# A hybrid decoder block on one core: the attention's second score product over 128 rows instead of 64

## The chip, the cores and the metric

The kernel runs on one core of a Trainium2 chip. The metric is the device time of one execution in microseconds (us); the median of three runs before the change is 2642.2 us (2641.92 to 2643.72). Lower is better. The core's engines are TensorE (PE in the profile, its weight loads PEld), VectorE (DVE), ScalarE (ACT), GpSimd (POOL) and SyncE (SP), which here only issues DMAs.

## The reference

One layer over 1024 tokens of width 1024, in float32. A mixer with two branches (stick-breaking attention and a gated linear recurrence, HGRN2), merged by gates, projected and normalized; then a mixture of experts (32 experts, 4 a token) and a second norm. The change concerns the attention's scores alone:

```python
for blk in range(T // SB_BLOCK):                 # 8 blocks of 128 queries, 8 heads of 64 channels
    t0, t1 = blk * SB_BLOCK, (blk + 1) * SB_BLOCK
    z = einsum('bhtd,bhsd->bhts', qf[:, :, t0:t1], kf[:, :, :t1]) * scale
    mask = arange(t1)[None, :] < (t0 + arange(SB_BLOCK))[:, None]
    log_keep = where(mask, log_sigmoid(-z), 0.0)
    log_after = cumsum(log_keep, axis=3, reverse=True) - log_keep
    weights = where(mask, exp(log_sigmoid(z) + log_after), 0.0)
    outs.append(einsum('bhts,bhsd->bhtd', weights, vf[:, :, :t1]))
```

## The kernel before

The program runs in stages, one after another: input projections, the recurrence beside some projections, the projections for the attention, the attention, the merge of the branches, the output projection with the router, the experts, the last norm. TensorE's float32 products are made from parts: each operand is split into a high and a low part of 12 bits (`split`, L124 to L126), and three products (high by high, high by low, low by high) are summed in one bank.

The attention is `sb_attention` (L557). A unit of work is one block of 128 queries for some heads: all 8 heads in block 0, 4 in block 1, 2 in blocks 2 and 3, and one head in blocks 4 to 7. There are 43 units, and block i has 128 * (i + 1) keys. A unit passes through four steps, one unit further behind in each: `scores` (matmuls L611 and L612, then on ScalarE a sigmoid of both signs, L615 and L616, then on GpSimd the mask, L620), `stick` (on VectorE a running product L629 and a product L631), `turn` (transposes on TensorE L642, copies L645 or L647) and `average` (matmuls L664 against the values).

The scores of a head take three part products, made in two matmuls for each stretch of up to 512 keys. A head has 64 channels, half of the 128 partitions. The tile `q` (`split_q`, L572) has the high part of a head's queries on the head's own half of the partitions and the low part on the other half; `kh` has the high part of its keys on both halves. So L611, over all 128 rows, makes high by high and low by high at once. What is left, queries high by keys low, is L612: it takes only the head's own 64 rows of `q` and of `kl`, in which two heads lie one below the other:

```python
r = slice(64 * (h % 2), 64 * (h % 2) + 64)
nc.tensor.matmul(o, q[:, h], self.kh[:, h, s], start=True, stop=False)
nc.tensor.matmul(o, q[r, h], self.kl[r, h // 2, s], start=False, stop=True)
```

So in a unit of one head with more than 512 keys four score matmuls follow one another, of 128, 64, 128 and 64 rows; with 8 heads in block 0 there are 16.

The queries come from DRAM. `load_q(i)` (L566) issues two DMAs on the SP queue into a tile `qraw`, of which there are two buffers. The first unit loads block 0 and block 1; every later block's first unit loads the next block. `split_q` (ScalarE copy L576, two VectorE subtractions L579) of the next block comes late in a block (in block 0 in its only unit, ahead of that unit's matmuls). The order in which instructions are written is the order on each engine.

Beside the attention runs a second stream of work, `beside` in `block_kernel` (L1643): first six pieces of the gates' projection (matmuls L130 to L132, 512 columns each; copies L548; weight loads on the SP queue L225, split by L125 and L126), then `turn_branches` (L696), which turns the branches' outputs (transposes L730, splits L125 and L126) once the memory of the projection has been given up. `lockstep` (L70) puts the two streams into one order by the estimated TensorE time that each piece yields. This order is fixed when the program is written, and does not hang on what the chip does.

Of the kernel before, what the change touches and what calls it, by code (L numbers as in the profile page):

```python
# [69 lines left out]
def lockstep(*streams):  # L70
    """Emits generators side by side; each yields the tensor-engine time of the piece it emitted."""
    total = [0.0] * len(streams)
    live = set(range(len(streams)))
    weight = [w for _, w in streams]
    gens = [g for g, _ in streams]
    while live:
        i = min(live, key=lambda j: total[j] / weight[j])
        try:
            total[i] += next(gens[i])
        except StopIteration:  # L80
            live.discard(i)


def shape_constants():
    """Arrays of zeros and ones that hang on the shapes alone."""
# [29 lines left out]
class Block:  # L115
# [56 lines left out]
    def scratch(self):  # L172
        """Expert lists in DRAM: (token, gate) by expert and place; at first every place names a zero row."""
        nc = self.nc
        self.tab_d = self.dram("tab_scratch", (NE * ROWS, 2), I32)
        self.h_d = self.dram("h_scratch", (ROWS, D))
        self.acc_d = self.dram("acc_scratch", (ROWS, D))
        n = NE * ROWS // 128
        for i in range(2):
            t = self.work.tile([128, n], I32, name="E0", bufs=EBUFS[0])  # L180
            nc.sync.dma_start(t, self.a["c_tab"][:, n * i:n * i + n])
            nc.gpsimd.dma_start(self.tab_d.rearrange("(p r) c -> p (r c)", p=128)[:, n * i:n * i + n], t)
        z = self.work.tile([128, 512], F32, name="E0", bufs=EBUFS[0])
        nc.gpsimd.memset(z, 0.0)
        for d in (self.h_d, self.acc_d):
            for half in range(2):
                nc.gpsimd.dma_start(d[T:T + 128, 512 * half:512 * half + 512], z)

# [1 line left out]
    def load_x(self):  # L190
        nc, a = self.nc, self.a
        # by half of the tokens
        self.xh = [p.tile([128, KT, 512], F32R, name=f"xh{i}") for i, p in enumerate(self.xpool)]
        self.xl = [p.tile([128, KT, 512], F32R, name=f"xl{i}") for i, p in enumerate(self.xpool)]
        # the place of q and f, which come later, takes the rows
# [21 lines left out]
    def fetch(self, col):  # L217
        """Loads columns col..col+256 of w_in and splits them."""
# [10 lines left out]
    def project(self, jobs, ahead=None):  # L229
        """jobs: (column, halves, evacuate): 256 columns by channel for these halves of the tokens, or by token for  # L230
        all of them where halves is None. A generator over pieces of tensor-engine work.

        ahead: a generator whose steps come before those of the first job.
        """
# [62 lines left out]
    def hgrn_jobs(self):  # L297
        """Projections of the HGRN branch: q^T and f^T by channel, v and the output gate by token."""
# [43 lines left out]
    def hgrn_chunks(self):  # L342
        """Chunks of 128 tokens: one chunk's decays beside the scores of the one before."""
# [17 lines left out]
    def hgrn_front(self, c, state):  # L361
        """Log gates of a chunk, their sums over ranges of tokens, and what these scale."""
# [15 lines left out]
        # q beside what the odd tokens' q keeps of the token before  # L378
# [10 lines left out]
        # decays from each token to the chunk's end  # L389
# [7 lines left out]
        for g, n in enumerate((4, 3)):  # L397
            for h in range(NH):
# [6 lines left out]
                for i in range(n):  # L405
# [5 lines left out]
                    # the first half of each block takes k, the second q  # L411
# [7 lines left out]
    def hgrn_back(self, c, state):  # L419
        """Scores within a chunk, its output, and the state it leaves."""  # L420
# [8 lines left out]
        # a token with itself and with the one before  # L429
# [52 lines left out]
    def rsqrt(self, pool, v, scale, eps, n):  # L482
        """1 / sqrt(v * scale + eps), with a Newton step on the table's value."""
# [14 lines left out]
    def sb_tiles(self):  # L498
        sp = self.spool
        # the first part of a head's keys lies on both halves of the partitions  # L500
        self.kh = sp.tile([128, SBH, T], F32R, name="kh")
        self.kl = sp.tile([128, 4, T], F32R, name="kl")
        self.sv = sp.tile([128, NB, 512], F32, name="sv")

    def sb_jobs(self):
        """q^T, kept in DRAM, k^T in two parts, v by token."""
# [33 lines left out]
    def gates_jobs(self):  # L540
        """The merge gates' arguments, by channel, kept in DRAM until the merge; a part of them early, a part late."""
# [15 lines left out]
    def sb_attention(self):  # L557
        """Weights sigmoid(z_s) * prod over s < s' < t of sigmoid(-z_s'), s < t."""
        nc, wk = self.nc, self.work
        self.os_d = self.dram("osb_scratch", (T, 512))  # L560
        # a unit is a head's block of queries, or several heads' where the keys are few
# [4 lines left out]
        def load_q(i):  # L566
            raw = wk.tile([128, SBH, 128], F32, name="qraw", bufs=2)
# [4 lines left out]
        def split_q(i):  # L572
            # the first part on the head's own partitions, the second on the others
# [7 lines left out]

        def heads(u):
            # those on the same half of the partitions follow one another: their products share a bank
# [4 lines left out]
        def scores(u):  # L588
            i, h0 = units[u]
            m, S = HEADS[i], 128 * (i + 1)  # L590
            if u == 0:
                load_q(i)
                split_q(i)
            if i in after and h0 == 0:
# [8 lines left out]
            for g in range(0, m, per):  # L603
                for s0 in range(0, S, 512):
                    n = min(512, S - s0)
                    ps = self.sps.tile([128, 512], F32, name="z", bufs=2)
                    for k in range(per):
                        h = hs[g + k]
                        r = slice(64 * (h % 2), 64 * (h % 2) + 64)
                        o, s = ps[:, S * k:S * k + n], slice(s0, s0 + n)  # L610
                        nc.tensor.matmul(o, q[:, h], self.kh[:, h, s], start=True, stop=False)  # L611
                        nc.tensor.matmul(o, q[r, h], self.kl[r, h // 2, s], start=False, stop=True)  # L612
# [4 lines left out]
            # a token keeps all of what itself and later ones would take  # L617
# [35 lines left out]
        def average(u):  # L653
            # two heads side by side, by channel
# [41 lines left out]
    def turn_branches(self):  # L696
        """The branches' outputs by channel, in two parts."""
# [4 lines left out]
        # the stick-breaking branch is there by channel: its own place in memory takes it  # L702
# [107 lines left out]
    def layer_norm(self, pool, r, st, g, b, out):  # L810
        """From the statistics of both halves of the rows."""
# [9 lines left out]
    def outproj(self):  # L821
# [6 lines left out]
        # the first part of the biases twice and the second, one below the other  # L828
# [33 lines left out]
        def add(tb, half):  # L862
            """The residual, and the statistics of what results."""
# [5 lines left out]
        def project(tbs):  # L869
            """Blocks of tokens; two at a time follow the loading of the weights row block by row block."""  # L870
# [26 lines left out]
        def route(tb):  # L897
# [10 lines left out]
            # four sums side by side, by expert, then their sum by token  # L908
# [17 lines left out]
            # which experts each token takes, and with what weight  # L926
# [31 lines left out]
            # places within the experts' lists  # L958
# [26 lines left out]
            # what the experts' outputs are added to: the residual and the weighted biases  # L985
# [36 lines left out]
        # then the last block first: the order of the experts waits for it  # L1022
# [11 lines left out]
    def expert_constants(self):  # L1034
        """What the sorting needs, and the biases in two parts, the second below the first."""
# [15 lines left out]
    def sort_experts(self):  # L1051
        """Each expert's place in the order of the counts."""
# [4 lines left out]
        # distinct keys: the count, then the lower expert first  # L1057
# [23 lines left out]
    def sort_biases(self):  # L1081
        nc, cp = self.nc, self.epool
        # biases of the first product, by channel and place in the order
# [11 lines left out]
    def list_beyond(self):  # L1095
        """What lies beyond the static sizes: blocks of 128 places, listed."""
# [15 lines left out]
        # row of an expert's first block beyond, less 128 for each block listed before  # L1112
# [4 lines left out]
        # one block a partition: its expert and its first row  # L1117
# [15 lines left out]
        # the same along a row  # L1133
# [14 lines left out]
    # Two forms of an expert's product. Up to 128 places: the tokens are the stationary operand and the  # L1148
    # weights stream past. More: the weights are stationary and both parts of the tokens stream past them.

    def expert(self, n, e, rows, bias, choice):
# [38 lines left out]
        def fetch(kind, c, q, width, queue=nc.sync, e=e):  # L1190
            """2048 weights a partition: a chunk of columns, blocks of rows from q * kr on."""
# [5 lines left out]
        def part(kind, c, q, width, kn):  # L1197
            """Piece q of a chunk of columns, kn blocks of rows, in two parts."""
# [156 lines left out]
        # pieces of work: the load of weights that starts with it, their split, the product, what follows a little later  # L1355
# [21 lines left out]
    def experts(self):  # L1377
# [12 lines left out]
        # an expert's second product follows the next one's first chunk, where their forms differ  # L1390
# [18 lines left out]
        # raw weights run ahead as far as there are places for them  # L1409
        places, ahead = [], [0]  # L1410

        def fetch(n=len(order)):
            """Weights for the pieces before n, while the last reader of the place to be filled is known."""
# [12 lines left out]
        def read(i):  # L1426
            """The piece's weights have been read."""
# [11 lines left out]
        # places in memory: what is written first lies where the stage before has long finished  # L1439
# [23 lines left out]
        def due(ts):  # L1463
            """What follows these pieces; tells if the tensor engine is in it."""
# [34 lines left out]
    def beyond(self):  # L1499
        """Blocks of 128 places beyond the static sizes, one after another."""  # L1500
# [18 lines left out]
    def load_rows(self):  # L1519
        """The last layer norm's two rows."""  # L1520
# [4 lines left out]
    def finish(self):  # L1525
# [30 lines left out]
        def by_scalar(tb):  # L1556
            """The mean, then the mean square of what is left."""
# [63 lines left out]
class Pools:  # L1621
    """Pools on the two stacks of the memory, opened and closed by name."""
# [129 lines left out]
```

## Time and profile before

| | |
|---|---|
| median of 3 runs | 2642.2 us (2641.92 to 2643.72) |
| profiled execution: first to last instruction | 2635.2 us |
| what lies around it, against the median | 7.0 us |
| TensorE busy | 2507.8 us (95%) |
| VectorE busy | 1865.8 us (71%) |
| ScalarE busy | 1452.9 us (55%) |
| GpSimd busy | 866.9 us (33%) |
| score matmuls L611 and L612 | 96 and 96, from 562.1 to 785.1 us |

The profiled execution's own time is told by its span; the 7.0 us beside it are taken from the median. A busy TensorE is not one at its peak: matmuls overlap, so the time from one start to the next (called the pitch here) is what counts, not the duration of one. An operand's form 64*128 means 64 rows by 128 columns of weights. The granted clock of TensorE (PEclk) is a share of full speed.

### The profile page before, as it was taken

How to read it: one execution, taken by the hardware profiler on the slowest of the kernel's cores; microseconds unless marked ns; L12 is line 12 of the kernel's file. 1: busy time of each engine (PE TensorE's matmuls, PEld its weight loads, DVE VectorE, ACT ScalarE, POOL GpSimd, SP SyncE). 2: the span in 40 equal slices, each digit the busy share in tenths (PEclk: the TensorE clock that was granted, in tenths of full speed). 3: DMA queues.
4: the chain of work that ended last, by engine and by line, in shares of the span. 5: the costliest groups of instructions: out<-in, count | busy, mean ns of one | idle time of the engine just before them, and what ended most of it. 6: DMA issues, size and time to landing. Idle time of an engine off the chain costs nothing. (4 is left out here: it accounts for less than half of the span.)

```text
span 2635.2 us, 41833 instructions
## 1 busy us (share of the span) xinstructions
PE 2507.8 (95%) x15476; PEld 2180.4 (83%) x15476; DVE 1865.8 (71%) x3091; ACT 1452.9 (55%) x2499; POOL 866.9 (33%) x742
## 2 busy tenths in 40 slices
PE   8999999999989995999999999999999999999992
PEld 8898888887767763988988999889988899888982
DVE  3227674347784576777788788887888888888785
ACT  3213332235563311666676677776777767777772
POOL 1010110013121233443434354434544434444443
PEclk9999999999999997999999999999999999999996
DMA  5321323233124524898998889999899998999973
GB/s 163 95 81 52 94 91 104 68 80 89 49 81 145 158 93 154 273 304 271 297 285 282 267 271 305 297 296 282 266 301 297 309 287 280 308 306 307 316 216 137
DMA packets 426788, 550.57 MB, mean 209 GB/s; under 512 B 21382, under 2 KB 312342, under 8 KB 426580
## 3 DMA queue, kind: packets, MB, share of 16 engines
q1 hardware_dynamic: 403684, 476.76, 56.1%
q0 software_dynamic: 22608, 70.05, 9.3%
q8 instruction: 123, 2.02, 0.3%
q10 hardware_dynamic: 288, 1.05, 0.1%
q14 instruction: 85, 0.70, 0.1%
HBM read 496.33 MB, written 51.47 MB: 208 GB/s over the span
## 5 line engine op out<-in xcount | busy, mean ns | idle before, releaser
L126 DVE TENSOR_TENSOR wl<-raw,wh 128x1024 fp32r<-128x1024 f32 x671 | 886.2, 1335 | 205.6 <-ACT wh L125 201.9
L125 ACT CAST wh<-raw 128x1024 fp32r<-128x1024 f32 x824 | 843.9, 1047 | 67.9 <-PE pj L269 20.6
L1216 PE MATMUL mm<-xTA,wh 128*128 128x292 f32 (+16 forms) x2304 | 617.5, 355 | 0.0
L126 POOL TENSOR_TENSOR wl<-raw,wh 128x1024 fp32r<-128x1024 f32 x153 | 377.3, 2466 | 541.1 <-ACT wh L125 481.6
L1218 PE MATMUL mm<-xTA,wl 128*128 128x146 f32 (+16 forms) x2304 | 545.0, 237 | 0.0
L1218 PEld LDWEIGHTS mm<-xTA,wl 128*128 128x128 f32 x2304 | 455.1, 198 | 0.5
L1216 PEld LDWEIGHTS mm<-xTA,wh 128*128 128x128 f32 x2304 | 450.8, 196 | 3.6 <-issue 2.7
L1265 PE MATMUL mm<-aTA,wh 128*128 128x292 f32 (+16 forms) x1152 | 300.4, 347 | 1.6 <-POOL aTA L126 1.6
L1267 PE MATMUL mm<-aTA,wl 128*128 128x146 f32 (+16 forms) x1152 | 270.9, 235 | 0.0
L1265 PEld LDWEIGHTS mm<-aTA,wh 128*128 128x128 f32 x1152 | 216.5, 188 | 5.6 <-POOL aTA L126 2.0
L1267 PEld LDWEIGHTS mm<-aTA,wl 128*128 128x128 f32 x1152 | 220.1, 191 | 0.0
L130 PE MATMUL pj<-xh,wh 128*128 128x512 f32 x512 | 209.4, 409 | 0.0
L126 POOL TENSOR_TENSOR aTA<-gl,aTA 128x146 fp32r<-128x146 f32 (+16 forms) x144 | 114.6, 803 | 285.9 <-ACT aTA L125 277.5
L132 PE MATMUL pj<-xh,wl 128*128 128x512 f32 x512 | 201.1, 393 | 0.0
L131 PE MATMUL pj<-xl,wh 128*128 128x512 f32 x512 | 200.7, 392 | 0.0
L1299 PE MATMUL mm<-wh,xTB 128*128 128x512 f32 x448 | 188.4, 420 | 0.0
L1301 PE MATMUL mm<-wh,xTB 128*128 128x512 f32 x448 | 176.3, 394 | 0.0
L1300 PE MATMUL mm<-wl,xTB 128*128 128x512 f32 x448 | 175.4, 391 | 0.0
L1225 ACT ACTIVATE gl<-mm,bup 128x146 f32<-128x146 f32 (+16 forms) x288 | 97.2, 389 | 134.1 <-PE mm L1218 132.4
L1235 DVE TENSOR_TENSOR gl<-gl 128x146 f32<-128x146 f32 (+16 forms) x144 | 107.4, 746 | 11.1 <-ACT gl L1234 10.9
L132 PEld LDWEIGHTS pj<-xh,wl 128*128 128x128 f32 x512 | 96.7, 189 | 21.3
L130 PEld LDWEIGHTS pj<-xh,wh 128*128 128x128 f32 x512 | 96.8, 189 | 20.8 <-issue 2.5
(346 smaller groups left out, 4671.5 us busy)
## 6 DMA issues: line engine op xcount, KB each, us to landing
raw<-in_expert_w_up_dram SPq DMA_DIRECT2D x252, 1024.0 KB, 5.9
raw<-in_expert_w_down_dram SPq DMA_DIRECT2D x128, 1024.0 KB, 7.0
raw<-in_w_in_dram SPq DMA_DIRECT2D x56, 512.0 KB, 5.3
gate_scratch<-pe POOLq DMA_DIRECT2D x32, 256.0 KB, 2.3
gate<-gate_scratch SPq DMA_DIRECT2D x8, 1024.0 KB, 5.1
qf<-in_x_dram SPq DMA_DIRECT2D x8, 512.0 KB, 8.1
qraw<-q_scratch SPq DMA_DIRECT2D x16, 256.0 KB, 4.6
xt<-in_x_dram SPq DMA_DIRECT2D x8, 512.0 KB, 3.5
```

The costliest lines, as they stand in the source:

```text
L125: nc.scalar.copy(hi, src)
L126: (engine or nc.vector).tensor_tensor(lo, src, hi.bitcast(F32), op=OP.subtract)
L130: nc.tensor.matmul(ps, wh, xh, start=start, stop=False)
L131: nc.tensor.matmul(ps, wh, xl, start=False, stop=False)
L132: nc.tensor.matmul(ps, wl, xh, start=False, stop=stop)
L1216: nc.tensor.matmul(ps[g][:, :2 * n], wh[:, kk, g::2], x[:, k].rearrange("p a n -> p (a n)"), start=k == 0, stop=False)
L1218: nc.tensor.matmul(ps[g][:, :n], wl[:, kk, g::2], x[:, k, 0], start=False, stop=k == KT - 1)
L1265: nc.tensor.matmul(ps[i][:, :2 * n], wh[:, kk, s], act[:, k].rearrange("p a n -> p (a n)"), start=k == 0, stop=False)
L1267: nc.tensor.matmul(ps[i][:, :n], wl[:, kk, s], act[:, k, 0], start=False, stop=k == KT - 1)
L1299: nc.tensor.matmul(p, x[:, k, 0], wh[:, kk], start=k == 0, stop=False)
L1300: nc.tensor.matmul(p, x[:, k, 0], wl[:, kk], start=False, stop=False)
L1301: nc.tensor.matmul(p, x[:, k, 1], wh[:, kk], start=False, stop=False)
```

## The change

Two tiles `qz` of four heads each are added. They hold the high part of the queries on the head's own half of the partitions and zeros on the other half. The zeros are written once by GpSimd, when the attention's tiles are made. For each block of queries the high parts are copied from `q` by ScalarE: `own_q(i, g)` is two copies of 64 partitions by 2 heads by 128 queries. L612 then takes all 128 rows of `qz` and of `kl`. Those rows of `kl` that belong to the other head meet zeros. `qraw` has one buffer instead of two, which gives back the memory of `qz`.

```diff
 def sb_tiles(self):
...
+        self.qz = [sp.tile([128, SBH // 2, 128], F32R, name=f"qz{i}") for i in range(2)]
+        for z in self.qz:
+            for k in range(2):
+                self.nc.gpsimd.memset(z[64 - 64 * k:128 - 64 * k, k::2].bitcast(F32), 0.0)
...
         def load_q(i):
-            raw = wk.tile([128, SBH, 128], F32, name="qraw", bufs=2)
+            raw = wk.tile([128, SBH, 128], F32, name="qraw", bufs=1)
...
+        def own_q(i, g):
+            for k in range(2):
+                r = slice(64 * k, 64 * k + 64)
+                nc.scalar.copy(self.qz[g][r, k::2], st["q", i][r, 4 * g + k:4 * g + 4:2].bitcast(F32))
...
         def scores(u):
...
             if u == 0:
                 load_q(i)
                 split_q(i)
+                own_q(i, 0)
+            if h0 == 0:
+                own_q(i, 1)
             if i in after and h0 == 0:
                 load_q(after[i])
             if i in after and h0 + m >= 6 and h0 < 6:
                 split_q(after[i])
...
-                        r = slice(64 * (h % 2), 64 * (h % 2) + 64)
                         o, s = ps[:, S * k:S * k + n], slice(s0, s0 + n)
                         nc.tensor.matmul(o, q[:, h], self.kh[:, h, s], start=True, stop=False)
-                        nc.tensor.matmul(o, q[r, h], self.kl[r, h // 2, s], start=False, stop=True)
+                        nc.tensor.matmul(o, self.qz[h // 4][:, h % 4], self.kl[:, h // 2, s], start=False, stop=True)
...
+            if i in after and h0 + m >= 6 and h0 < 6:
+                own_q(after[i], 0)
```

Comments and docstrings are removed as well, which changes no instruction.

## Rows read from the trace of the kernel before

**Rows 1.** The page's head: the span of the profiled execution.
```profile
span 2635.2 us, 41833 instructions
```

**Rows 2.** Busy time by stretch: stretch, length, engines' busy us (instructions), granted clock, DMA.
```profile
562.00:602.00 40.00, 38.00 (x184) 27.08 (x184) 30.39 (x42) 19.26 (x36) 13.18 (x16) 0.91 0.58 135
577.40:602.20 24.80, 22.90 (x137) 16.11 (x136) 23.74 (x29) 14.01 (x28) 9.82 (x12) 1.00 0.55 135
602.00:738.00 136.00, 136.00 (x828) 95.95 (x827) 103.22 (x99) 78.17 (x170) 32.95 (x69) 1.00 0.21 60
738.00:798.00 60.00, 46.65 (x367) 34.10 (x366) 48.05 (x43) 36.30 (x72) 14.86 (x20) 0.91 0.33 101
754.80:792.70 37.90, 30.11 (x228) 21.43 (x227) 37.01 (x32) 25.73 (x52) 11.63 (x15) 0.91 0.17 56
```

**Rows 3.** TensorE in order of time, a unit of block 3: start, us, instruction, count.
```profile
611.63 0.40 PE L131 MATMUL pj<-xl,wh 128*128 128x512 f32 x1
611.86 0.40 PE L132 MATMUL pj<-xh,wl 128*128 128x512 f32 x1
612.10 0.39 PE L611 MATMUL z<-kh,q 128*128 128x512 f32 x1
612.42 0.50 PE L612 MATMUL z<-kl,q 64*128 64x512 f32 x1
612.85 0.49 PE L611 MATMUL z<-kh,q 128*128 128x512 f32 x1
...
613.70 0.88 PE L642 MATMUL wt<-idn,take 128*128 128x128 f32 x6
614.33 0.48 PE L130 MATMUL pj<-xh,wh 128*128 128x512 f32 x1
```

**Rows 4.** The same view: six transposes that no score matmul precedes.
```profile
700.66 0.82 PE L642 MATMUL wt<-idn,take 128*128 128x128 f32 x6
701.23 0.48 PE L611 MATMUL z<-kh,q 128*128 128x512 f32 x1
```

**Rows 5.** The same view: a unit of block 4, 512 and 128 keys.
```profile
629.78 0.39 PE L611 MATMUL z<-kh,q 128*128 128x512 f32 x1
...
631.04 1.09 PE L642 MATMUL wt<-idn,take 128*128 128x128 f32 x8
```

**Rows 6.** The same view, in the experts: a bias product of 64 rows.
```profile
2519.33 0.50 PE L1304 MATMUL mm<-bupr,permr 64*128 64x512 f32 x1
2519.76 0.40 PE L1216 MATMUL mm<-xTA,wh 128*128 128x268 f32 x1
```

**Rows 7.** Groups, weight loads in 602 to 738: count, busy us, mean ns, idle before.
```profile
L131 PEld LDWEIGHTS pj<-xl,wh 128*128 128x128 f32 x76 | 14.4, 189 | 1.7
```

**Rows 8.** Groups, ScalarE in 602 to 738: the copy nearest in size.
```profile
L647 ACT COPY wt<-wt 128x256 f32<-128x256 f32 x8 | 3.2, 396 | 0.0
```

**Rows 9.** The page's DMA issues: count, KB each, median us to landing.
```profile
qraw<-q_scratch SPq DMA_DIRECT2D x16, 256.0 KB, 4.6
```

**Rows 10.** SP queue in order of time: a load of queries at the start.
```profile
562.83 1.84 SPq L569 DMA_DIRECT2D qraw<-q_scratch  x2
```

**Rows 11.** ScalarE in order of time, start of the attention; the releaser in brackets.
```profile
556.89 1.05 ACT L576 CAST q<-qraw 128x1024 fp32r<-128x1024 f32 x1 [1.49 <-DMA qraw<-q_scratch]
557.96 1.28 ACT L615 ACT_TABLE_LOAD   x1
564.24 0.60 ACT L615 ACTIVATE keep<-z 128x512 f32<-128x512 f32 x1 [5.00 <-PE z L612]
```

**Rows 12.** VectorE in order of time, the same stretch.
```profile
561.35 2.84 DVE L579 TENSOR_TENSOR q<-qraw,q 64x512 fp32r<-64x512 f32 x4
568.82 3.50 DVE L629 TENSOR_TENSOR_SCAN keep<-keep,one 128x128 f32<-128x128 f32 x8 [4.63 <-POOL keep L620]
572.43 1.22 DVE L631 TENSOR_TENSOR take<-take,keep 128x1016 f32<-128x1016 f32 x1
577.41 0.69 DVE L548 COPY pe<-pj 128x512 f32<-128x512 f32 x1 [3.77 <-PE pj L132]
```

**Rows 13.** TensorE in order of time, after the gates' projection.
```profile
748.29 0.63 PE L730 MATMUL pj<-idn,ot 128*128 128x128 f32 x4 [3.62 <-DMA ot<-ohg_scratch]
```

## The prediction, made before the change was run

> **What bounds the kernel now.** I read the page first: one core, TensorE busy nearly everywhere, a span of 2635.2 us [rows 1]. The change touches only the attention, so I cut that stage into stretches and asked for the busy time of each engine [rows 2]. Three regimes show. From 577.4 to 602.2 VectorE is busy 23.74 of 24.8 us: it goes from one instruction to the next, and TensorE runs two units behind it and can't pull it. From 602 to 738, while pieces of the gates' projection lie between the units, TensorE has no idle time at all (136.00 of 136.00) and VectorE 103.22. From 754.8 to 792.7 VectorE is busy again without a break (37.01 of 37.9), with block 7's long running products. So a TensorE saving is worth its size only in the middle stretch.
>
> Then I read the starts of TensorE's matmuls one by one there [rows 3]. The reader is to look at the distance between starts, not at durations. Full-row matmuls of 512 columns follow at 0.23 us (611.63, 611.86, 612.10: 0.235 on the mean). From the first score matmul on it is 0.32 (612.10 to 612.42) and then 0.43 (612.42 to 612.85) for the same 512 columns: each passage between 128 and 64 rows costs some 0.2 us. The operands are not the reason: in the experts another product of 64 rows, L1304, also holds up what follows for 0.43 us [rows 6].
>
> **The change part by part.**
>
> *Pitch of the scores.* With L612 over 128 rows nothing switches within a unit. A unit of block 3 has four score matmuls of 512 columns: 612.10 to 613.70 is 1.60 us, against 4 x 0.235 = 0.94; saved 0.66. The six transposes behind it take 0.63 us (613.70 to 614.33) against 0.57 where no score matmul precedes [rows 3, 4]; another 0.06. Together 0.72 us a unit. In block 4, with 512 and 128 keys, 629.78 to 631.04 is 1.26 us [rows 5]; two at 0.235 and two at 0.095 (a transpose of 128 columns, 0.57 / 6) would be 0.66, saved 0.60, with the transposes' share 0.66. I take 0.72 for the units of the other widths, since the switch, not the width, is what is paid. From 602 to 738 there are 28 units: the last of block 2, four of block 3, eight each of blocks 4 and 5, seven of block 6. 20 x 0.72 + 8 x 0.66 = 14.4 + 5.3 = 19.7 us. Bounds: nothing, if it isn't the rows; 112 matmuls x 0.2 = 22.4.
>
> *A rule against this.* The trace shows weight loads of 189 ns for full-row matmuls that start every 0.235 us [rows 3, 7]: 0.189 and 0.213 (512 columns at 2.4 GHz) don't fit into that one after the other, so the load runs beside the matmul ahead of it, on the same rows. The Trainium skill, "TensorE: Matmul & The Clock Gate", section "Part 3: Packing small matmuls — row/col tiling", says that a weight load overlaps matmuls in flight only where the row groups differ. By that rule the change would save nothing, since full rows always share their groups, and the sum's first term would be 0 instead of -19.7. The trace does not agree for the full-row matmuls of this kernel.
>
> *ScalarE's copies.* 32 copies of 64 partitions x 256, at 0.396 us by the nearest row (128x256) [rows 8]: 12.7 us in all. In 602 to 738 there are some 20, 7.9 us, on top of 78.17 of 136 us [rows 2]: in the 118 us that I expect there, 73% busy. They follow sigmoids that have already waited for the last reader of the half of `qz` that they overwrite, so they wait for nothing; behind them in ScalarE's queue the unit's next sigmoid comes 0.8 us later. Nothing, with up to 0.8 us for each of five blocks if that cover fails (4.0).
>
> *The zeros.* Four memsets on GpSimd before the scores; GpSimd is idle for most of the time ahead of the attention. Nothing; at most 1.4 us.
>
> *One buffer of qraw: the start.* Block 1's queries now wait until block 0's have been split on VectorE, whose first pair of subtractions (of the four at 561.35) is over at 562.8 [rows 12]. A load that waits for just this stands in the trace: 562.83 [rows 10]. Two issues later and 4.6 us [rows 9] it lands near 568.0. ScalarE's copy of block 1 (1.05) and, as now, the table load (1.28) stand ahead of the first sigmoid [rows 11]: 570.3 instead of 564.24, 6.0 late. On the SP queue the weights' loads stand behind the waiting one, but they are needed only ten and more us later. The running products then start near 573.1 instead of 568.82; with 4.83 us for them and L631 they end at 577.9, where VectorE now sits idle from 573.65 to 577.41 [rows 12]. That idle time swallows all but 0.5 us. TensorE waits as well: block 1's `qz` is copied behind block 0's four sigmoids (0.60 each at most) and is ready near 573. Then come 8 scores of 256 columns (half of 0.235 each) and 12 gate matmuls, until 576.8; at half clock, which part of this stretch already has (0.91 granted over 40 us, so 7.2 us at the lower of the two levels) [rows 2], until 580. So VectorE begins its unbroken run 0.5 to 2 us late, and TensorE's savings up to 602 (16 x 0.165 in block 0, and seven units' worth of 0.72: 7.6) go into waiting for it; two or three units' worth of them make up for the delay. I take 0 at 602, between +6.0 (all late) and -7.6 (all saved). The later loads of queries wait for splits half a block before; they have the other half.
>
> *VectorE behind a faster TensorE.* It needs 103 of what becomes 116 us: 89%. Bursts, such as the weights' splits between the running products, will now stop TensorE sometimes. I put +2 us, between 0 and +10 (then VectorE would be only 82% busy, 103.2 / 126).
>
> *After 738.* The last gate matmul frees the memory into which the branches' outputs are loaded, so this stretch begins with the shift gained and then runs as before: TensorE waits for that DMA at 748.29 [rows 13], and from 754.8 on VectorE is full. Nine units' savings (9 x 0.72 = 6.5) lie under these. 0, between -6.5 and +1.
>
> Sum: -19.7 + 0 + 2 + 0 = -17.7. The profiled span of 2635.2 becomes 2617.5; with the 7.0 us that the median has more than the span, 2624.5 us. All later stages are shifted as they are.
>
> **The rivals.**
>
> *VectorE becomes the bound.* For it: 23.74 of 24.8 us busy in 577 to 602, and 89% afterwards. Against it: the steps of a unit lie a unit apart, so VectorE works ahead of the transposes. If it can be kept only 80% busy, 602 to 738 lasts 129 us, the gain is 7: with something of the start 2632 to 2637.
>
> *More is saved.* If the start loses nothing (its 7.6 saved) or the end follows TensorE, the gain is 22 to 34: 2608 to 2620. Against it: the unbroken VectorE stretches.
>
> *The pitch is not of the rows, and the start is paid in full: slower.* The place is the beginning of the attention: 6.0 us late there, not absorbed because TensorE also idles and runs the 12 gate matmuls at half clock (12 x 0.2 = 2.4). That gives +8.4, 2650.6 us. It decides if a score matmul saves under 8.4 / 112 = 0.075 us. For it: each score matmul's extra time, 0.19 to 0.2, is also the length of a weight load [rows 7], so a weight load that can't be hidden for some other reason would look the same. Against it: rows 3 and 6.
>
> *The two cancel.* A start paid in full with VectorE-bound blocks behind it: 2638 to 2646.
>
> **How the numbers follow.** The forecast (2618 to 2630) 0.62; VectorE the bound 0.16; more saved 0.11; cancelled 0.07; slower 0.04. A difference under 0.2%, 5.3 us, can't be told from none. Faster takes the first three, 0.89; same 0.07; slower 0.04. The range leaves out the top of "cancelled" and "slower", and the lower part of "more saved": 2614 to 2634.
>
> **What would show it.** In the changed profile: score matmuls of 512 columns at a pitch near 0.235 in blocks 3 to 7, and 0.12 or so for 256; the stretch from the last unit of block 2 to the last gate matmul some 116 to 120 us long, VectorE near 90% in it; ScalarE's first sigmoid 5 to 6 us later than 564.24 and the first gate copy within 3 us of 577.41; the time from the last gate matmul to the merge's first unchanged at some 60 us. I am wrong if the pitch stays at 0.43, if TensorE shows waits of more than some 5 us in all for VectorE in the middle stretch, or if the end shortens.

## The result, and the profile after

The changed kernel takes 2624.1 us (median of 4 runs, 2621.57 to 2625.72) against 2642.8 us before (4 runs, 2641.92 to 2643.72): 18.7 us less, a ratio of 0.993 [0.9916, 0.9944]. The forecast was 2624.5 us.

The head of the page after, for [rows 1]. From one span to the other it is 13.1 us, 5.5 less than the medians say; why comes below.

```profile
span 2622.1 us, 41858 instructions
```

TensorE in order of time, the unit of block 3 of [rows 3] (the lines of the code have moved: L611 and L612 are now L623 and L624):

```profile
613.23 0.39 PE L623 MATMUL z<-kh,q 128*128 128x512 f32 x1
613.46 0.39 PE L624 MATMUL z<-kl,qz 128*128 128x512 f32 x1
613.68 0.39 PE L623 MATMUL z<-kh,q 128*128 128x512 f32 x1
613.91 0.40 PE L624 MATMUL z<-kl,qz 128*128 128x512 f32 x1
614.15 0.82 PE L656 MATMUL wt<-idn,take 128*128 128x128 f32 x6
614.72 0.48 PE L130 MATMUL pj<-xh,wh 128*128 128x512 f32 x1
...
628.59 0.40 PE L623 MATMUL z<-kh,q 128*128 128x512 f32 x1
628.82 0.39 PE L624 MATMUL z<-kl,qz 128*128 128x512 f32 x1
629.05 0.22 PE L623 MATMUL z<-kh,q 128*128 128x128 f32 x1
629.11 0.28 PE L624 MATMUL z<-kl,qz 128*128 128x128 f32 x1
629.23 0.95 PE L656 MATMUL wt<-idn,take 128*128 128x128 f32 x7
```

Read the distance between starts. Four scores take 613.23 to 614.15, 0.92 us (1.60 before), and the six transposes 0.57 (0.63 before): 0.74 us saved in the unit, 0.72 forecast. The last five lines are the unit of block 4 of [rows 5]: 0.64 us instead of 1.26. The matmuls of 512 columns last 0.39 to 0.40 us now; before, the ones at a passage lasted 0.49 to 0.50 [rows 3].

Where the time of a passage goes is seen in TensorE's weight loads at the same places, before and after:

```profile
612.42 0.18 PEld L612 LDWEIGHTS z<-kl,q 64*128 64x128 f32 x1 [0.36 <-issue]
612.85 0.19 PEld L611 LDWEIGHTS z<-kh,q 128*128 128x128 f32 x1 [0.25 <-issue]
```

```profile
613.23 0.19 PEld L624 LDWEIGHTS z<-kl,qz 128*128 128x128 f32 x1
613.46 0.19 PEld L623 LDWEIGHTS z<-kh,q 128*128 128x128 f32 x1
```

Before, the load for a matmul starts with that matmul (612.42 and 612.85, as in [rows 3]). After, it starts one matmul ahead: the load at 613.23 is for the matmul at 613.46, and it runs beside the matmul of 613.23. So the extra 0.2 us of a passage fits a load of 0.18 to 0.19 us that nothing hides. Why a load doesn't run ahead where the number of rows changes, no run shows.

Busy time by stretch (columns as in [rows 2]): the start, the middle up to the last gate matmul, and from there to the first matmul of the merge.

```profile
562.00:602.00 40.00, 29.40 (x169) 24.02 (x170) 28.84 (x39) 23.95 (x46) 11.76 (x14) 0.87 0.36 88
602.00:721.50 119.50, 118.54 (x848) 96.92 (x845) 106.19 (x102) 84.47 (x188) 42.60 (x71) 1.00 0.32 88
721.50:783.30 61.80, 45.46 (x368) 37.32 (x366) 48.54 (x44) 38.22 (x76) 17.68 (x22) 0.83 0.33 105
```

In the middle TensorE is still nearly full (118.54 of 119.50) with VectorE at 106.19, 89% as forecast. At the end the granted clock is 0.83; in the kernel before the last stage of the attention had 0.91 [rows 2].

The start: ScalarE, VectorE and TensorE in order of time, for [rows 11, 12].

```profile
555.39 1.05 ACT L581 CAST q<-qraw 128x1024 fp32r<-128x1024 f32 x1 [14.32 <-DMA qraw<-q_scratch]
556.47 1.68 ACT L590 CAST qz<-q 64x256 fp32r<-64x256 f32 x4
569.46 1.04 ACT L581 CAST q<-qraw 128x1024 fp32r<-128x1024 f32 x1 [11.31 <-DMA qraw<-q_scratch]
570.52 1.28 ACT L627 ACT_TABLE_LOAD   x1
571.81 0.60 ACT L627 ACTIVATE keep<-z 128x512 f32<-128x512 f32 x1
```

```profile
574.67 4.33 DVE L643 TENSOR_TENSOR_SCAN keep<-keep,one 128x128 f32<-128x128 f32 x8 [2.73 <-POOL keep L634]
579.11 1.22 DVE L645 TENSOR_TENSOR take<-take,keep 128x1016 f32<-128x1016 f32 x1
580.45 0.69 DVE L553 COPY pe<-pj 128x512 f32<-128x512 f32 x1
```

```profile
563.26 0.33 PE L623 MATMUL z<-kh,q 128*128 128x128 f32 x1 [1.24 <-DVE q L584]
...
572.95 0.58 PE L623 MATMUL z<-kh,q 128*128 128x256 f32 x1 [4.90 <-ACT take L628]
```

ScalarE stands idle for 11.31 us until block 1's queries arrive in the one buffer, and the first sigmoid comes at 571.81 instead of 564.24. TensorE then waits 4.90 us. The first score starts at 563.26 here and at 562.10 before; that much lies ahead of the attention and differs between profiled runs of either form (561.55 to 563.39), so I count from the first score.

Four stages laid end to end, each from the start of one matmul to the start of another in the trace (us). The first runs from the first score to the first score of block 2's last unit (before 601.43, after 604.12), the second to the last gate matmul (737.70, 721.61), the third to the merge's first matmul (797.96, 783.35), the fourth to the end of the span:

| | start | middle | end of the attention | later stages | sum |
|---|---|---|---|---|---|
| before | 39.33 | 136.27 | 60.26 | 1837.2 | 2073.1 |
| after | 40.86 | 117.49 | 61.74 | 1838.8 | 2058.8 |
| difference | +1.5 | -18.8 | +1.5 | +1.5 | -14.3 |

The change's whole gain lies in the middle; a few us of it are lost around it. With the 1.16 us of the first score these make the 13.1 us between the spans.

### The profile page after: what moved, and what is told of

Its sections match the earlier page's. It is cut to its first block, busy times and chain, and to the rows that moved or that the text cites. A ratio compares the mean times of both kernels' runs of the same rounds, so it can differ in the third digit from the quotient of the medians.

```text
span 2622.1 us, 41858 instructions
## 1 busy us (share of the span) xinstructions
PE 2482.2 (95%) x15476; PEld 2182.3 (83%) x15476; DVE 1866.3 (71%) x3091; ACT 1464.9 (56%) x2531; POOL 880.9 (34%) x746
## 5 line engine op out<-in xcount | busy, mean ns | idle before, releaser
L1362 POOL DMA_INDIRECT acc_scratch<-yo,ti x50 | 99.3, 1986 | 42.2 <-ACT yo L1302 16.8
```

## The experiments

My theory: the passages between 128 and 64 rows cost the time, their removal gives the 18.8 us of the middle, and the start loses to the single buffer about what the scores save there. Rivals: 64-row matmuls are slow by themselves; the start costs more than its savings; the gain is lost at the end. The profiled runs have some 1.6 us around the span, and each comparison of times has its own runs of before.

**Before once more.** No edit; for the difference between the spans and the medians.

> The kernel before, unchanged, for a profile on the same chip as the others. The first profile of it has a span of 2635.2 us, 7.0 under the median of its timed runs, while the changed kernel's profile lies 2.0 under its median. If the first profile was simply a quick execution, this one shows a span of 2638 to 2642 us with the additional 3 to 6 us spread over the stages after the attention; if 7 us really lie around the span, it shows 2635 again.

Measured: 2640.34 us, span 2638.7. From the first score to the last gate matmul it is 175.69 us (175.60 in the first trace), but the later stages take 1839.2 instead of 1837.2. Over all traces these untouched stages lie between 1837.2 and 1843.8. So the first profiled execution of before was a quick one (2635.2 + 1.6 is 2636.8, where the median was 2642.2), and the attention's own difference is what its stages show.

**The cost alone.** The changed kernel, but the second product takes 64 rows again; copies, zeros and the one buffer stay.

```diff
-nc.tensor.matmul(o, self.qz[h // 4][:, h % 4], self.kl[:, h // 2, s], start=False, stop=True)
+r = slice(64 * (h % 2), 64 * (h % 2) + 64)
+nc.tensor.matmul(o, q[r, h], self.kl[r, h // 2, s], start=False, stop=True)
```

> All that the change adds (zeros, the 32 copies on ScalarE, one buffer for the raw queries), but the second product still takes 64 rows of q and of the keys' low part. Theory (the rows are what pays, the additions cost only at the start): score matmuls of 512 columns stay at a pitch of 0.43 us; the first sigmoid comes 5 to 7 us later than in the kernel before, VectorE's unbroken run 1 to 3 us later; time 1 to 3 us above the kernel before, 2643.5 to 2646. Rival (the start is paid in full): 6 to 9 us above, 2649 to 2652. Rival (the idle time of VectorE swallows all): no difference, within 0.5 us.

Measured: 2643.06 us (10 runs) against 2640.79 (13), ratio 1.0008 [0.9998, 1.0017]; not told apart from no change. In the trace the first sigmoid is 8.22 us behind the first score (2.14 before), but block 2's last unit only 41.99 behind it (39.33 before): 2.7 us of the 6.1 arrive, within the 1 to 3 us expected. The middle takes 136.3 us, as before: the work of the copies costs nothing there. Nothing reads `qz` in this kernel, so a wait for the copies could not show; in the changed kernel TensorE waits for them once, 0.66 us at the start, and never in the middle.

**The passages halved, the rows kept.** The kernel before; in blocks 2 to 7, where no two heads share a bank of scores, the 128-row matmuls of both banks come first, then both of 64 rows. The operations are the same, only their order differs.

```diff
+banks = [(g, s0, min(512, S - s0)) for g in range(0, m, per) for s0 in range(0, S, 512)]
+for part in ([banks] if per == 1 else [[x] for x in banks]):
+    pss = [self.sps.tile([128, 512], F32, name="z", bufs=2) for _ in part]
+    jobs = [(x, ps, k) for x, ps in zip(part, pss) for k in range(per)]
+    order = [(*j, low) for low in range(2) for j in jobs] if per == 1 else [(*j, low) for j in jobs for low in range(2)]
+    for (g, s0, n), ps, k, low in order:
...
+        if low:
             nc.tensor.matmul(o, q[r, h], self.kl[r, h // 2, s], start=False, stop=True)
+        else:
+            nc.tensor.matmul(o, q[:, h], self.kh[:, h, s], start=True, stop=False)
```

> The kernel before, with the order of a unit's score matmuls changed in blocks 2 to 7: first both of 128 rows, then both of 64 rows. The same instructions, two passages between row counts in a unit instead of four. Theory (the passage costs): the two 64-row matmuls follow each other at 0.235 us like full-row ones, a unit saves about half of its 0.72 us, 28 units of the middle stretch some 10 us; time 2632 to 2636. Rival (a 64-row matmul is slow by itself, before and behind it): 0.43 us between the two as well, one slow pitch of four gone, 0.2 x 28 = 5.6 us; time about 2637. Rival (it is neither): no difference.

Measured: 2629.88 us, ratio 0.9956 [0.994, 0.9973], 10.9 us less. The middle takes 124.61 us, 11.7 less than before; 28 units with two passages fewer make 0.42 us a unit on the mean. Counted from the first score to the transposes, the 23 units of one head save 0.39 each, so 0.2 a passage, as [rows 3] gave; the five of two heads save some 0.6, because their two 64-row matmuls also run side by side (last section). TensorE in order of time, a unit of block 6 with both 64-row matmuls (512 and 384 columns) on the same half (1.09 us to the transposes; 1.51 before), and a unit of block 3 with two heads, so on opposite halves:

```profile
703.70 0.56 PE L615 MATMUL z<-kh,q 128*128 128x512 f32 x2
704.19 0.67 PE L613 MATMUL z<-kl,q 64*128 64x512 f32 x2
704.79 0.66 PE L646 MATMUL wt<-idn,take 128*128 128x128 f32 x4
...
611.23 0.62 PE L615 MATMUL z<-kh,q 128*128 128x512 f32 x2
611.78 0.50 PE L613 MATMUL z<-kl,q 64*128 64x512 f32 x2
612.21 0.87 PE L646 MATMUL wt<-idn,take 128*128 128x128 f32 x6
```

On the same half the two take 0.60 us to the next instruction, the passage out included; a 64-row matmul by itself held up what follows for 0.43 us [rows 6], so a second one adds only 0.17. So 64 rows are not slow, the passage is: that rival falls. Some 10 us less were expected if the passage costs, 5.6 by the rival.

**The start mended.** The changed kernel, but block 1's raw queries go into a buffer of `take`, which is free at that time, so that they don't wait for block 0's.

```diff
-raw = wk.tile([128, SBH, 128], F32, name="qraw", bufs=1)
+if i == BLOCKS[1]:
+    raw = wk.tile([128, T], F32, name="take", bufs=4).rearrange("p (h t) -> p h t", h=SBH)
+else:
+    raw = wk.tile([128, SBH, 128], F32, name="qraw", bufs=1)
```

> The changed kernel, with block 1's raw queries loaded into a free buffer of the tile that later holds the weights, so that this load need not wait for block 0's split. Theory (the wait at the start costs 2 to 3 us, since VectorE's unbroken run begins that much later): first sigmoid 564 to 567 us, the first gate copy 3 us earlier than in the changed kernel, the time 2 to 4 us below it, 2620 to 2622. Rival (the wait is hidden): 2624, no difference to the changed kernel.

Measured: 2618.02 us (2615.32 to 2620.56), ratio 0.9907 [0.9888, 0.9926], 22.8 us less than before. The interval overlaps that of the change; the trace decides. ScalarE and VectorE in order of time:

```profile
558.59 1.05 ACT L584 CAST q<-take 128x1024 fp32r<-128x1024 f32 x1
...
564.54 0.60 ACT L630 ACTIVATE keep<-z 128x512 f32<-128x512 f32 x1 [3.60 <-PE z L627]
```

```profile
567.39 3.89 DVE L646 TENSOR_TENSOR_SCAN keep<-keep,one 128x128 f32<-128x128 f32 x8 [1.90 <-POOL keep L637]
571.39 1.40 DVE L648 TENSOR_TENSOR take<-take,keep 128x1016 f32<-128x1016 f32 x1
572.70 0.68 DVE L553 COPY pe<-pj 128x512 f32<-128x512 f32 x1
```

The first gate copy comes 9.31 us behind the first score (before 15.31, after 17.19), and block 2's last unit 34.21 behind it (39.33, 40.86). So against the change the start gives 6.6 us back, where 2 to 3 were expected, and the middle is the same (117.45 us against 117.49). This version beats the kernel before; against the changed kernel it is the trace of the start that shows the gain.

**Which blocks carry the gain.** In one kernel only blocks 3 to 6 have full rows, in the other only 0, 1, 2 and 7; in both the one buffer stays, and copies are made only for the blocks named.

```diff
+if i in (3, 4, 5, 6):      # the other kernel: (0, 1, 2, 7)
     nc.tensor.matmul(o, self.qz[h // 4][:, h % 4], self.kl[:, h // 2, s], start=False, stop=True)
+else:
+    r = slice(64 * (h % 2), 64 * (h % 2) + 64)
+    nc.tensor.matmul(o, q[r, h], self.kl[r, h // 2, s], start=False, stop=True)
```

> The changed kernel, but only blocks 3 to 6 take the second product over 128 rows (27 of the 28 units of the middle stretch, 56% of the score matmuls); blocks 0 to 2 and 7 take 64 rows as before, without copies into qz. Theory (a TensorE saving counts only between the last unit of block 2 and the last gate matmul): nearly the whole gain stays, 15 to 18 us below the kernel before; that stretch 117 to 119 us; from the last gate matmul to the merge's first 60 to 61 us. Rival (every score matmul counts alike): 56% of 18.7, so 10.5 us below.

> The opposite: only blocks 0 to 2 and 7 over 128 rows, blocks 3 to 6 with 64 rows. Theory: one unit of the middle stretch saved (0.7 us), the start 1 to 3 us late, the end 1 to 2 us longer: 0 to 4 us above the kernel before. Rival (every score matmul counts alike): 44% of 18.7, 8 us below.

Measured: blocks 3 to 6 alone, 2626.11 us against 2643.3 (13 runs), ratio 0.9932 [0.9915, 0.9948], 17.2 us less: nearly the whole gain. The others alone, 2642.17 us, 0.9997 [0.9988, 1.0007]: none that can be told. From the first score to the last gate matmul: 160.09 us with blocks 3 to 6, 158.35 with all, 176.65 with the others alone, 178.28 in the kernel with the cost alone. Either way the full rows of blocks 0 to 2 are worth some 1.7 us here, of which block 2's last unit has its 0.7 in the middle. With the one buffer, then, most of the 7.6 us that the prediction worked out for the start is lost in waiting, as it said. (Blocks 3 to 6 have 112 of the 192 score matmuls, 58%, so the rival's gain is 10.9 us; it falls with either figure.)

**The end with block 7 at 64 rows.** The mended kernel, with the same edit of the matmul as above and the list of blocks (0, 1, 2, 3, 4, 5, 6); the copies are made for all blocks. A single execution, so its time decides nothing.

> The changed kernel with the mended start, but block 7 with 64 rows, so that TensorE is as busy behind the last gate matmul as in the kernel before. In the changed kernel this stretch is 61.7 us at a granted clock of 0.83, before 60.3 at 0.91. Theory (less TensorE work there means more time at the lower clock, and transposes on the way to VectorE take longer for it): 60 to 61 us again, clock near 0.9; rival (something else made it longer): 61.7 to 62.3.

Measured: 2617.11 us (2618.02 for the mended kernel); the last gate matmul is 151.30 us behind the first score (151.66 in the mended kernel). Busy time from the last gate matmul to the merge, first the mended kernel, then this one:

```profile
715.00:777.30 62.30, 45.80 (x368) 37.66 (x367) 48.53 (x44) 38.21 (x76) 17.27 (x22) 0.84 0.33 104
```

```profile
714.30:775.00 60.70, 46.99 (x368) 34.88 (x366) 48.40 (x44) 37.85 (x76) 15.08 (x22) 0.89 0.33 107
```

The stretch is 1.6 us shorter (60.61 against 62.24 between the matmuls), at a higher granted clock. So far this fits the account that shorter scores leave TensorE idle more often, so that more of the rest runs at the lower of its two levels. But the kernel with full rows in 0, 1, 2 and 7 takes 60.30 us here, also at 0.89, with full rows in block 7. Two traces with full rows in both block 7 and blocks 3 to 6 have 61.7 and 62.2 us; the seven others with the same gate pieces, before's two included, lie between 60.1 and 60.9. Whether it takes both, or single profiles differ that much, stays open.

**More gate work beside the end.** The mended kernel with the weight that the two streams' order is made with at 0.50 instead of 0.57, so that pieces of the gates' projection come later.

```diff
-LW2 = 0.57
+LW2 = 0.50
```

> The changed kernel with the mended start, and the second stream's weight in the order of the two set to 0.50 instead of 0.57, so that the gates' projection is spread over more units of the attention. Theory (the middle is bound by TensorE and the end by VectorE): fewer gate matmuls ahead of block 6 take TensorE's load there, VectorE gets to some 95%; but the branches' outputs are then turned later, and the end hangs on them: between 5 us less and 5 us more than with the start mended alone. Rival (the split of the two streams does not matter, since all work has to be done): within 1 us of it.

Measured: 2622.78 us (2621.65 to 2625.79), ratio 0.992 [0.9903, 0.9936], 20.5 us less than before. In the traces the last gate matmul comes 169.15 us behind the first score and the merge 48.81 behind that: 217.96 in all, where the mended kernel has 151.66 + 62.24 = 213.90. TensorE's two longest waits from 602 to 800 (what is waited for: us in total, times, longest), the mended kernel and this one:

```profile
PE wt L659 <- DVE take L648: 6.1, 4, 2.2
PE pj L747 <- DMA ot<-ohg_scratch: 4.6, 1, 4.6
```

```profile
PE wt L659 <- DVE take L648: 16.5, 9, 3.9
PE pj L747 <- DMA ot<-ohg_scratch: 6.7, 1, 6.7
```

The later pieces reach into block 7, where VectorE's long running products set the pace: TensorE waits 16.5 us for them instead of 6.1. Ahead of block 6 VectorE is 87% busy (77.96 of 89.75 us), where 95% was expected. At this weight, then, the pieces don't fill TensorE's spare time at the end; they bring VectorE their copies and splits too.

## Why the prediction was right, and where its terms were off

*The pitch of the scores: right.* Forecast 0.72 and 0.60 us for a unit of blocks 3 and 4 (0.66 with the transposes' share in the latter), measured 0.74 and 0.62. Over 28 units 19.7 us were forecast; the middle got 18.8 shorter, and the 0.9 between them is the size of the one wait below. The grouped kernel shows the mechanism apart from the number of rows. By the weight loads shown above, the extra time of a score matmul is a load that isn't hidden, as the prediction's slower rival had suspected; but it comes with the passage between row counts and is gone where all rows are equal. The weight loads of the second product last 188 ns in the middle stretch, with score matmuls of 512 columns 0.23 us apart (count, busy us, mean ns, idle before):

```profile
L624 PEld LDWEIGHTS z<-kl,qz 128*128 128x128 f32 x56 | 10.5, 188 | 1.7
```

The rule of the Trainium skill that was weighed ("TensorE: Matmul & The Clock Gate", "Part 3: Packing small matmuls — row/col tiling"), taken alone, would have left the middle as it was. The trace after disagrees with it: the loads at 613.23 and 613.46 above run beside matmuls on the same rows.

*VectorE behind a faster TensorE: +2 forecast, 0.9 measured.* It is 89% busy, and yet TensorE waits for it once between 602 and 721.5:

```profile
PE wt L656 <- DVE wt L659: 0.9, 1, 0.9
```

The pipeline of units does what the argument against that rival said: VectorE works ahead of the transposes.

*The start: 0 forecast, +1.5 measured.* The chain was right: block 1's copy at 569.46 (landing forecast at 568.0), the first sigmoid 6.4 us later than before when counted from the first score (6.0; 7.6 by the profile's clock, outside the 5 to 6 given as a sign), the first gate copy 1.9 us later counted so, and 3.04 by the profile's clock, just over the 3 given. With the one buffer the savings of blocks 0 to 2 do go into waiting.

What the prediction did not weigh is what that buffer hides. Ahead of its unbroken run VectorE waits for TensorE: 3.77 us before 577.41, released by the gate matmuls [rows 12]. So what TensorE saves ahead of that point brings the whole run forward, unless the queries come late. With the buffer mended the run starts 7.9 us earlier than in the changed kernel (9.31 against 17.19), and the start is 6.6 us shorter than after and 5.1 shorter than before, near the forecast's bound of -7.6 for "all saved". I had put the 0 in the middle of the bounds and treated the run as a limit. The run itself is hardly shorter in any of them: from the first gate copy to block 2's last unit it is 24.0 us before, 23.7 after and 24.9 mended.

Not all of this is the pitch. Busy time of a stretch just behind the first scores, before and in the mended kernel (columns as in [rows 2]):

```profile
564.90:571.40 6.50, 6.50 (x17) 4.95 (x17) 2.58 (x6) 1.51 (x3) 2.15 (x2) 0.50 1.09 255
```

```profile
563.39:568.02 4.63, 4.63 (x29) 4.15 (x30) 2.67 (x4) 3.42 (x8) 1.76 (x2) 1.00 0.54 119
```

Before, the first 12 gate matmuls run at the lower level of TensorE's clock (granted 0.50) and take 5.07 us; in the mended kernel they run at the higher one (1.00) and take 2.79. In all five traces with full rows in block 0 they run at the higher level, in the five others at the lower; in the changed kernel the lower level falls on the next gate matmuls, behind the wait for the queries. Up to block 1's first score the mended kernel takes 5.2 us less than before (4.63 against 9.88). An estimate from these starts gives the clock some 3 us of it: 2.3 in the gate matmuls, and 0.7 in block 0's last five scores, which before start every 0.40 us instead of every 0.255.

*After 738: 0 forecast, +1.5 measured.* The DMA's wait is there as forecast, on the transposes that were L730:

```profile
731.53 1.09 PE L744 MATMUL pj<-idn,ot 128*128 128x128 f32 x4 [4.27 <-DMA ot<-ohg_scratch]
754.18 1.08 PE L656 MATMUL wt<-idn,take 128*128 128x128 f32 x4 [1.74 <-DVE take L645]
```

Then VectorE holds TensorE, so block 7's savings vanish (60.30 us with full rows in blocks 0, 1, 2 and 7 alone, 60.43 with the cost alone), and the stretch ends 1.5 us longer at a granted clock of 0.83; the cause of the 1.5 stays open, as above.

*Copies and zeros: right.* The copies take 403 ns on the mean (396 forecast), 16 of them in the middle (some 20 forecast), and TensorE never waits for them there; the memsets run at 429 us, long before.

*Span and median.* The sum of -17.7 was set on a span of 2635.2, and 7.0 us were added as what lies around it. Only 1.6 lies around it; the other 5.4 is that this execution was quicker than the median, 2.0 of it against a second trace in the later stages alone. The forecast of the median came out right all the same, since the 7.0 stood for the whole step from that execution to the median: 18.7 us were measured between the medians, while the trace shows 15.8 us for the three stages of the attention (18.8 - 1.5 - 1.5). The 2.9 us between these are within what single profiles differ by. So that forecast and median agree to 0.4 us is in part luck: in the trace the middle gained 1.1 us more than forecast, and the start and the end lost 1.5 each that had been put at nothing.

*The rivals.* VectorE as the bound falls with the 0.9 us of waiting; "not of the rows" with the grouped kernel and the weight loads; a start paid in full with the cost alone, of whose 6.1 us 2.7 arrive at block 2. "More is saved" is what another kernel, the one with the mended start, gives: 2618.0 us, within the 2608 to 2620 put on it, for the reason named there, a start that loses nothing.

## What to carry to other kernels

Where matmuls over all rows and over half of them alternate, look at the distance between starts: a passage cost some 0.2 us here (0.15 with 128 columns), so zeros in the other half, or just an order that puts equal row counts together, was worth more than the smaller operand. Count such a saving only where TensorE is what the others wait for; where another engine runs without a break, it goes into waiting, but look for what that engine waits for just ahead of its run. And when a buffer is given back to pay for it, look at the one moment when both were in use: here the single `qraw` took 4.1 us of 22.8 by the medians, whose intervals overlap, and 6.6 us in the traces, and a buffer of `take` that is idle at that time gives them back.

## What the runs showed that I had not expected

Two 64-row matmuls of 512 columns on opposite halves of the rows cost no more than one: in the grouped kernel's block 3 the two take 611.78 to 612.21, 0.43 us, the time that one alone holds up the next instruction [rows 6], where two on the same half take 0.60 us (with 512 and 384 columns). With 128 columns the passage weighs most beside the matmul itself: block 0's scores follow each other every 0.11 us after the change and every 0.255 before at the same granted clock, as these lines of before show:

```profile
562.10 0.33 PE L611 MATMUL z<-kh,q 128*128 128x128 f32 x1 [1.24 <-DVE q L579]
562.35 0.32 PE L612 MATMUL z<-kl,q 64*128 64x128 f32 x1
562.61 0.33 PE L611 MATMUL z<-kh,q 128*128 128x128 f32 x1
```
